# Seven homes for raw pieces from the last query job on, a top-16 over 80 of 256 pairs, and queries copied by ScalarE

## The chip, the cores and the metric

One core of one Trainium2 chip. The metric is the device time of one execution in microseconds; the kernel before was timed in three runs. The engines are TensorE (PE; its weight loads are PEld), VectorE (DVE), ScalarE (ACT), GpSimd (POOL) and SyncE (SP), each with a queue that it works through in order, and 16 DMA engines that carry the transfers of all of them.

## What is computed

A decoder layer for 256 tokens of width 1024: three gated token mixers, their merge, and a feed-forward part in which every token picks its experts by product keys. The change touches this last part. Cut to what matters:

```python
q = (hi @ w_q).reshape(B, T, 8, 2, 128)
s = einsum('bthpd,hpkd->bthpk', q, subkeys)          # 128 keys, two halves, 8 heads
s_top, i_top = top_k(s, 16)
cand = s_top[..., 0, :, None] + s_top[..., 1, None, :]          # 16 x 16 pairs
best, pos = top_k(cand.reshape(..., 256), 16)
expert = i_top[0][pos // 16] * 128 + i_top[1][pos % 16]
g = softmax(best)
a = gelu(einsum('btd,bthkd->bthk', hi, u_tab[expert]))
y = einsum('bthk,bthkd->btd', g * a, v_tab[expert])
```

`hi` is the RMS-normalised stream; both expert tables have 16384 rows of 1024 numbers (64 MB each).

## The kernel before

**Raw pieces.** Weights and both expert tables come as pieces of 128 x 1024 float32, two to a transfer of 1 MB (`load_raw`, L65 to L71, on SyncE's queue). A transfer lands in a home, a tile of the pool `rawp` with three of them. 82 pieces `w` serve the projections; each is split by ScalarE (L202) and VectorE or GpSimd (L203) into two parts, which TensorE multiplies in three products (L233 to L235). Then come 128 pieces `u` and 128 pieces `v`, which TensorE uses as they are. `ahead_split` (L260) is called before every job: it splits pieces up to two jobs ahead and issues transfers up to `more["depth"]` pieces beyond that, which is two at first.

**Queries.** The last 16 `w` jobs (66 to 81) make the queries of 8 heads x 2 halves. `ev_pq` (L828) moves each from PSUM, times the token's RMS factor. `scores` (L864) multiplies them with the keys; four at a time are copied to `sc` (L872).

**The order of the selection.** What VectorE does for the selection stands in lists `todo` of (cost, function); `tick2` and `run_todo` (L881) put a purse's worth of them into the program after each job: 1.5 in a query job, `SEL_PACE` = 1.85 in a `u` job. First all of the upper 128 tokens (t = 1), then the lower (t = 0): `top_keys` (16 of 128 keys, costed 1.4), then by rounds of heads `sel_a` (the 256 pair sums), `sel_b` (`top16` of them, costed 2.4 a head), `sel_p` (position to row and column), `sel_d` (their key numbers), and at the end `sel_c`, `sel_x` (exponential, on ScalarE), `sel_c2`, `sel_e` (transposes on TensorE). `select` (L1226) writes that list. These are no times: the purse only says where in VectorE's queue a function stands.

**Tokens in two ways.** For the upper 96 tokens the chosen rows of both tables are gathered (`x_load`, L1036, an indirect transfer of 128 rows, 512 KB, on GpSimd's queue; 96 of the first table, then 96 of the second) into six buffers, the former homes of the split parts; VectorE takes each in `x_step` (L1052: product with the token; L1057: weighted sum) and the next transfer is issued as its buffer is free. Their list has a purse of its own, `X_PACE`: 0.35 a `u` job before the gates, 1.3 after, with 1.2 as the cost of a step. For the other 160 tokens every expert is multiplied: `u_job` (L1108) makes 128 x 160 inner products of a piece `u` on TensorE, ScalarE takes their GELU; `v_job` (L1132) multiplies a piece `v` with the weights and adds up in PSUM.

**The gates.** When both halves of the selection are through, `open_gates` (L1239) gives back the room of the selection, opens three more homes (`raw2`, six in all, depth five), and from there 40 gate steps (`g_prep`, `g_gi`, `g_mm`, `g_copy`, `g_apply`) spread the chosen weights over the 128 x 160 table beside the remaining `u` jobs, at a rate of 40 steps in the jobs up to number 124.

Of the kernel before, what the change touches and what calls it, by code (L numbers as in the profile page):

```python
# [10 lines left out]
F32 = mybir.dt.float32  # L11
F32R = mybir.dt.float32r
BF = mybir.dt.bfloat16
F16 = mybir.dt.float16
I32 = mybir.dt.int32
U32 = mybir.dt.uint32
AF = mybir.ActivationFunctionType
OP = mybir.AluOpType
# [20 lines left out]
N_WARM = 12  # L39
SEL_PACE = 1.85  # L40
X_PACE = (0.35, 1.3)
RAW_BUFS = 3
# [5 lines left out]
def hybrid_block(ctx, tc, xt, memt, wst, cmpw, subk, cols, cpe, fng, ut, vt, un, out):  # L48
    nc = tc.nc
    const = ctx.enter_context(tc.tile_pool(name="const", bufs=1))  # L50
    big = ctx.enter_context(tc.tile_pool(name="big", bufs=1))
    hb = ExitStack()
    far = hb.enter_context(tc.tile_pool(name="far", bufs=1, side="right"))
    hbp = hb.enter_context(tc.tile_pool(name="hbp", bufs=1, side="right"))
    rawp = ctx.enter_context(tc.tile_pool(name="rawp", bufs=RAW_BUFS))
# [4 lines left out]

    raws, more = {}, {"from": None, "depth": RAW_BUFS - 1}

    nc.scalar.preload_act_table_set("natural_log_exp_and_others")

    def load_raw(r):  # L65
        kind, i = raw_list[r]
        pool = rawp if more["from"] is None or (r - more["from"]) // RAW_BUFS % 2 else more["pool"]
        t = pool.tile([128, 2, 1024], F32, name="raw")
        src = {"w": wst, "u": ut, "v": vt}[kind]
        nc.sync.dma_start(t, src[2 * i:2 * i + 2].rearrange("n p c -> p n c"))  # L70
        raws[r] = t  # L71
# [26 lines left out]

    nc.sync.dma_start(xT[:, 0:2], xt[:, 0:2])
    raw0 = rawp.tile([128, 2, 1024], F32, name="raw")  # L100
    raws[0] = raw0
# [724 lines left out]
    qt_ = {}  # L826

    def ev_pq(i):  # L828
        def f(p):
            qt_[i] = far.tile([128, T], F32, name=("pq0", "pq1", "rxb")[i]) if i < 3 else \  # L830
                sel.tile([128, T], F32, name=f"pq{i % 3}")
            nc.vector.tensor_tensor(qt_[i], p, rmsf[1], op=OP.mult)
        return f
# [11 lines left out]
    def norm_h(d):  # L845
# [11 lines left out]
    nc.gpsimd.iota(io2, pattern=[[1, 128], [0, 2]], base=0, channel_multiplier=0,  # L857
                   allow_small_or_imprecise_dtypes=True)
    se = ExitStack()
    sel = se.enter_context(tc.tile_pool(name="sel", bufs=1, side="right"))  # L860
# [65 lines left out]
    def sel_a(t, hs):  # L926
        if ("tf", t) not in sd:
            sel_open(t)
            nc.vector.tensor_copy(sd["tf", t], ti[t])
        sd["c", t] = sel.tile([128, len(hs), 16, 16], F32, name="cand")  # L930
        a = tv[t].rearrange("p (h s) k -> p h s k", s=2)
        for n, h in enumerate(hs):
            nc.vector.tensor_tensor(sd["c", t][:, n], a[:, h, 0, :, None].to_broadcast([128, 16, 16]),
                                    a[:, h, 1, None, :].to_broadcast([128, 16, 16]), op=OP.add)

    def sel_b(t, h, n):
        top16(sd["bv", t][:, h], sd["bi", t][:, h], sd["c", t][:, n].rearrange("p a b -> p (a b)"))

# [4 lines left out]
    def sel_p(t, hs):  # L943
        pp = sel.tile([128, 2, len(hs), 16], U32, name="pp")
        bi = some(sd["bi", t], hs)
        nc.vector.tensor_scalar(pp[:, 0], bi, 4, None, op0=OP.logical_shift_right)
        nc.vector.tensor_scalar(pp[:, 1], bi, 15, None, op0=OP.bitwise_and)
        nc.vector.tensor_copy(some(sd["pf", t], hs, 2), pp)

# [18 lines left out]
    def sel_x(t):  # L968
        nc.scalar.activation(sd["bv", t], sd["bv", t], AF.Exp)
        todo[t].append((1.1, lambda: sel_c2(t)))  # L970
# [255 lines left out]
    def select(t):  # L1226
        w = todo[t]
        for hs, parts in (X_ROUNDS if t else (((0, 1, 2, 3), 0), ((4, 5, 6, 7), 0))):
            w.append((0.35 * len(hs), lambda hs=hs: sel_a(t, hs)))
            for n, h in enumerate(hs):  # L1230
                w.append((2.4, lambda h=h, n=n: sel_b(t, h, n)))
            w.append((0.6, lambda hs=hs: sel_p(t, hs)))
            for s in range(2):
                w.append((0.1 + 0.75 * len(hs), lambda hs=hs, s=s: sel_d(t, s, hs)))
            if t:
                w.append((0.3, lambda hs=hs, parts=parts: x_index(hs, parts)))
        w.append((0.6, lambda: sel_c(t)))

    def open_gates():  # L1239
        nonlocal gp  # L1240
        se.close()
        hb.close()
        gp = ctx.enter_context(tc.tile_pool(name="gp", bufs=2))
        rc = ctx.enter_context(tc.tile_pool(name="rc", bufs=1))
        slots["RC"] = rc.tile([128, 64, ND], F32, name="RC")
        more["pool"] = ctx.enter_context(tc.tile_pool(name="raw2", bufs=RAW_BUFS))
        more["from"], more["depth"] = next_raw[0], 2 * RAW_BUFS - 1
        g_prep(0)

    gp, q, opened, rate, owed, late = None, 0, False, 0.0, 0.0, None  # L1250
    for i in range(128):
# [20 lines left out]
        if i < 4:  # L1272
            x_rows(i % 2, i > 1)
        if not opened:
            tick2(SEL_PACE if i < 90 else 1e9)
            opened = len(sel_done) == 2
            if opened:
                open_gates()
                g_gi(0)
                rate = N_G / (124.0 - i)  # L1280
# [140 lines left out]
```

## Time and profile before

| | us |
|---|---|
| median of 3 runs (lowest, highest) | 956.25 (955.26, 956.61) |
| the profiled execution, own time | 955.32 |
| its span, first to last instruction | 953.6 |
| TensorE busy | 913.3 (96%) |
| VectorE busy | 629.9 (66%) |
| ScalarE busy | 340.0 (36%) |
| GpSimd busy | 310.6 (33%) |

The span is what all times below are counted in; the rest of the profiled execution's time lies around it. TensorE's products overlap, so that its busy share says little about how fast it goes; the number of its records in a stretch says more (16 records are one `u` or `v` job). In all 285.17 MB go through the DMA engines, a mean of 299 GB/s. The granted clock of TensorE is 0.994 on average. The stages by the trace: projections and mixers up to about 260, query jobs to 308, `u` jobs to 634, `v` jobs to 930, the rest to 953.6.

### The profile page before, as it was taken

The page shows a single profiled execution, that of the slowest core. Times are in us where ns is not written, and L with a number is a line of the kernel's source. Part 1 is how long each engine was busy: PE and PEld are TensorE (multiplying, and loading weights), DVE is VectorE, ACT ScalarE, POOL GpSimd, SP SyncE. Part 2 cuts the span into 40 slices and gives each one's busy share as a digit, 9 for nine tenths or more (in the row PEclk, how much of TensorE's full clock was granted, in tenths as well). Part 3 has the DMA queues.
Part 4 walks back from the last instruction along what each step waited for, and adds up shares of the span by engine and source line. Part 5 has one row for each costly group of instructions (what it writes and reads, how often), then busy time and mean ns, then how long its engine had stood idle before and what let it go on. Part 6 is the DMA issues. An engine that isn't in the chain of part 4 may idle for free.

```text
span 953.6 us, 17339 instructions
## 1 busy us (share of the span) xinstructions
PE 913.3 (96%) x6807; PEld 870.3 (91%) x6807; DVE 629.9 (66%) x1375; ACT 340.0 (36%) x918; POOL 310.6 (33%) x343
## 2 busy tenths in 40 slices
PE   8999999998999999999999999999999998999996
PEld 6999999898999999999999989899999888888895
DVE  7757668657779969999687778874444444444412
ACT  4754679654533312113777667620000000000001
POOL 7802000026842044112344334343333333333200
PEclk9999999999999999999999999999999999999998
DMA  7644434443553499898999999999999999999951
GB/s 284 248 133 144 135 135 148 155 138 133 178 176 133 164 362 329 302 324 304 410 408 408 409 409 407 409 402 409 409 409 409 409 408 409 409 409 409 409 234 45
DMA packets 76324, 285.17 MB, mean 299 GB/s; under 512 B 6881, under 2 KB 6929, under 8 KB 75857
## 3 DMA queue, kind: packets, MB, share of 16 engines
q1 hardware_dynamic: 47152, 181.15, 50.7%
q0 software_dynamic: 28800, 102.61, 27.4%
q8 instruction: 54, 0.88, 0.4%
q10 hardware_dynamic: 288, 0.29, 0.1%
q14 instruction: 30, 0.24, 0.1%
HBM read 282.63 MB, written 1.05 MB: 297 GB/s over the span
## 4 chain that ended last, share of the span: by engine, by line
PE 48%; DMA 19%; issue 12%; DVE 10%; POOL 8%; ACT 2%; POOLq 0%; SPq 0%; DVEq 0%
DMA raw<-in_vt_dram 16%; PE po L1129 16%; POOL s L1043 7%; PE pj L233 6%; PE pj L235 6%; PE pj L234 6%; PE pj L1114 5%; DVE s L1052 1%; DMA s<-in_un_dram,xi 1%; DVE s L203 1%; ACT gi L1156 1%; POOL t L783 1%; DMA xi<-e 1%; DVE ti L902 1%; DVE sc L903 1%
## 5 line engine op out<-in xcount | busy, mean ns | idle before, releaser
L1114 PE MATMUL pj<-hA,raw 128*128 128x160 f32 x2048 | 290.3, 301 | 3.0 <-DMA raw<-in_ut_dram 2.4
L1114 PEld LDWEIGHTS pj<-hA,raw 128*128 128x128 f32 x2048 | 281.2, 191 | 7.2 <-issue 2.4
L1057 DVE SCALAR_TENSOR_TENSOR acc<-s,xw,acc 128x1024 f32<-128x1024 f32 x94 | 120.8, 1285 | 130.4 <-DMA s<-in_vt_dram,xi 124.5
L1043 POOL DMA_INDIRECT s<-in_un_dram,xi x96 | 104.4, 1087 | 187.0 <-DVE xa L1052 136.4
L1129 PE MATMUL po<-RC,raw 128*128 128x160 f32 x1024 | 148.0, 302 | 11.7 <-DMA raw<-in_vt_dram 10.6
L1129 PEld LDWEIGHTS po<-RC,raw 128*128 128x128 f32 x1024 | 140.1, 190 | 19.2 <-DMA raw<-in_vt_dram 15.9
L1129 PE MATMUL po<-RA,raw 128*128 128x160 f32 x1024 | 141.9, 300 | 3.4 <-DMA raw<-in_vt_dram 3.4
L1043 POOL DMA_INDIRECT s<-in_vt_dram,xi x96 | 91.5, 954 | 164.7 <-DVE acc L1057 152.4
L1129 PEld LDWEIGHTS po<-RA,raw 128*128 128x128 f32 x1024 | 139.4, 190 | 5.8 <-DMA raw<-in_vt_dram 5.8
L1052 DVE CUSTOM_DVE_ANT_0 s<-s,hA 128x1024 f32<-128x1024 f32 x96 | 116.9, 1221 | 29.4 <-DMA s<-in_un_dram,xi 26.4
L203 DVE TENSOR_TENSOR s<-raw,s 128x1024 fp32r<-128x1024 f32 (+1 forms) x77 | 100.9, 1316 | 28.5 <-ACT s L202 28.2
L202 ACT ACTIVATE s<-raw 128x1024 fp32r<-128x1024 f32 (+1 forms) x84 | 86.5, 1034 | 68.4 <-PE pj L234 47.1
L1156 ACT ACTIVATE gi<-oo,gv 128x128 f16<-128x128 f16 x320 | 99.3, 426 | 13.6 <-DVE oo L1145 12.7
L1204 ACT ACTIVATE RA<-pg 128x512 f32<-128x512 f32 x2 | 1.2, 593 | 281.5 <-PE pg L1306 281.5
L233 PE MATMUL pj<-hA,s 128*128 128x256 f32 x336 | 99.0, 295 | 0.1
L235 PE MATMUL pj<-hA,s 128*128 128x256 f32 x336 | 95.0, 283 | 0.0
L234 PE MATMUL pj<-hA,s 128*128 128x256 f32 x336 | 95.0, 283 | 0.0
L233 PEld LDWEIGHTS pj<-hA,s 128*128 128x128 f32 x336 | 64.3, 191 | 3.3 <-issue 1.8
L234 PEld LDWEIGHTS pj<-hA,s 128*128 128x128 f32 x336 | 64.3, 191 | 0.6 <-issue 0.5
L235 PEld LDWEIGHTS pj<-hA,s 128*128 128x128 f32 x336 | 64.2, 191 | 0.0
L1118 ACT ACTIVATE RA<-pj 128x160 f32<-128x160 f32 x64 | 19.3, 303 | 112.9 <-PE pj L1114 111.0
L781 POOL TENSOR_TENSOR t<-t,t 128x256 f32<-128x256 f32 x7 | 5.2, 736 | 106.1 <-DVE t L780 106.1
(347 smaller groups left out, 1248.7 us busy)
## 6 DMA issues: line engine op xcount, KB each, us to landing
raw<-in_ut_dram SPq DMA_DIRECT2D x64, 1024.0 KB
raw<-in_vt_dram SPq DMA_DIRECT2D x64, 1024.0 KB
raw<-in_wst_dram SPq DMA_DIRECT2D x39, 1024.0 KB
raw<-in_wst_dram SPq DMA_DIRECT2D x4, 512.0 KB
s<-in_un_dram,xi POOLq DMA_INDIRECT x96
s<-in_vt_dram,xi POOLq DMA_INDIRECT x96
x<-in_memt_dram SPq DMA_DIRECT2D x1, 1024.0 KB
cw<-in_cmpw_dram POOLq DMA_DIRECT2D x1, 1024.0 KB
```

What stands on the lines that cost most here:

```text
L202: nc.scalar.activation(a[:, c], src[:, c], AF.Copy)
L203: eng.tensor_tensor(b[:, c], src[:, c], a[:, c].bitcast(F32), op=OP.subtract)
L233: nc.tensor.matmul(dst, l1, r1, start=first, stop=False)
L234: nc.tensor.matmul(dst, l1, r2, start=False, stop=False)
L235: nc.tensor.matmul(dst, l2, r1, start=False, stop=last)
L1043: nc.gpsimd.indirect_dma_start(t, None, src, bass.IndirectOffsetOnAxis(ap=xi[:, c:c + 1], axis=0))
L1052: nc.vector.tensor_tensor_reduce(t, t, hnat[:, g], 1.0, 0.0, OP.mult, OP.add, xa[:, c:c + 1])
L1057: nc.vector.scalar_tensor_tensor(acc[:, g], t, xw[:, c:c + 1], acc[:, g], op0=OP.mult, op1=OP.add)
L1114: nc.tensor.matmul(p, a[:, k], hT[:, k, 0:ND], start=(k == 0), stop=(k == 7))
L1118: nc.scalar.activation(slot(i)[:, g:], p[:, g:], AF.Gelu)
L1129: nc.tensor.matmul(po[c // 2][:, c % 2], a[:, c * 128:c * 128 + 128], slot(i), start=(i == 0 and c % 2 == 0), stop=(i == 127), skip_group_ ...
L1156: nc.scalar.activation(gi[:, s, k // 2, :, k % 2], oo[:, k // 2, :, k % 2], AF.Copy, scale=gv[:, q, s, k:k + 1])
```

## The change

- **Homes.** `more["homes"]` is a list that turns: each transfer takes the home at its head and puts it at the end; the depth is one less than their number. Two homes of `raw2` are added once the third query is made, and two more after `u` job 0, in the room of the tiles `hB1` and `hB2`, which held the input of the query jobs. The gates open none.
- **Selection.** Of the 16 x 16 pairs (a, b) only 80 are formed: all b for a = 0, b below 8 for a = 1 to 7, b = 0 for a = 8 to 15. `sel_p` turns a position among 80 back into a row and a column with six more instructions.
- **Queries** are copied by ScalarE and not multiplied by the RMS factor; the factor is put into the exponential instead.
- **Paces and costs.** `SEL_PACE` 1.75, `X_PACE` (0.45, 1.3), and other costs for `sel_a`, `sel_b` and `sel_p`.

```diff
-SEL_PACE = 1.85
-X_PACE = (0.35, 1.3)
+SEL_PACE = 1.75
+X_PACE = (0.45, 1.3)
...
+    hbp = ctx.enter_context(tc.tile_pool(name="hbp", bufs=1, side="right"))
     hb = ExitStack()
     far = hb.enter_context(tc.tile_pool(name="far", bufs=1, side="right"))
-    hbp = hb.enter_context(tc.tile_pool(name="hbp", bufs=1, side="right"))
...
-    raws, more = {}, {"from": None, "depth": RAW_BUFS - 1}
+    raws, more = {}, {"homes": [(rawp, "raw")] * RAW_BUFS, "depth": RAW_BUFS - 1}
+
+    def add_homes(new):
+        more["homes"] = new + more["homes"]
+        more["depth"] = len(more["homes"]) - 1
...
-        pool = rawp if more["from"] is None or (r - more["from"]) // RAW_BUFS % 2 else more["pool"]
-        t = pool.tile([128, 2, 1024], F32, name="raw")
+        homes = more["homes"]
+        homes.append(homes.pop(0))
+        t = homes[-1][0].tile([128, 2, 1024], F32, name=homes[-1][1])
...
-            nc.vector.tensor_tensor(qt_[i], p, rmsf[1], op=OP.mult)
+            nc.scalar.activation(qt_[i], p, AF.Copy)
...
+    raw2 = ctx.enter_context(tc.tile_pool(name="raw2", bufs=2))
+    add_homes([(raw2, "raw")] * 2)
...
-        sd["c", t] = sel.tile([128, len(hs), 16, 16], F32, name="cand")
-        a = tv[t].rearrange("p (h s) k -> p h s k", s=2)
-        for n, h in enumerate(hs):
-            nc.vector.tensor_tensor(sd["c", t][:, n], a[:, h, 0, :, None].to_broadcast([128, 16, 16]),
-                                    a[:, h, 1, None, :].to_broadcast([128, 16, 16]), op=OP.add)
+        n = len(hs)
+        c = sel.tile([128, n, 80], F32, name="cand")
+        sd["c", t] = c
+        v = some(tv[t].rearrange("p (h s) k -> p h s k", s=2), hs)
+        nc.vector.tensor_tensor(c[:, :, 0:16], v[:, :, 0, 0:1].to_broadcast([128, n, 16]), v[:, :, 1], op=OP.add)
+        nc.vector.tensor_tensor(c[:, :, 16:72].rearrange("p h (a b) -> p h a b", b=8),
+                                v[:, :, 0, 1:8, None].to_broadcast([128, n, 7, 8]),
+                                v[:, :, 1, None, 0:8].to_broadcast([128, n, 7, 8]), op=OP.add)
+        nc.vector.tensor_tensor(c[:, :, 72:80], v[:, :, 0, 8:16], v[:, :, 1, 0:1].to_broadcast([128, n, 8]), op=OP.add)
...
-        nc.vector.tensor_scalar(pp[:, 0], bi, 4, None, op0=OP.logical_shift_right)
-        nc.vector.tensor_scalar(pp[:, 1], bi, 15, None, op0=OP.bitwise_and)
-        nc.vector.tensor_copy(some(sd["pf", t], hs, 2), pp)
+        nc.vector.tensor_scalar(pp[:, 0], bi, 3, None, op0=OP.logical_shift_right)
+        nc.vector.tensor_scalar(pp[:, 1], bi, 7, None, op0=OP.bitwise_and)
+
+        y = sel.tile([128, 6, len(hs), 16], F16, name="py")
+        row, c = y[:, 0], y[:, 1]
+        nc.vector.tensor_copy(y[:, 0:2], pp)
+        nc.vector.tensor_scalar(y[:, 2], c, 8.0, None, op0=OP.add)
+        nc.vector.scalar_tensor_tensor(y[:, 3], row, 9.0, y[:, 2], op0=OP.is_ge, op1=OP.mult)
+        nc.vector.scalar_tensor_tensor(some(sd["pf", t][:, 0], hs), row, 1.0, y[:, 3], op0=OP.subtract, op1=OP.max)
+        nc.vector.scalar_tensor_tensor(y[:, 4], row, 9.0, c, op0=OP.is_lt, op1=OP.mult)
+        nc.vector.tensor_scalar(y[:, 5], row, 1.0, 8.0, op0=OP.is_equal, op1=OP.mult)
+        nc.vector.tensor_tensor(some(sd["pf", t][:, 1], hs), y[:, 4], y[:, 5], op=OP.add)
...
-        nc.scalar.activation(sd["bv", t], sd["bv", t], AF.Exp)
+        nc.scalar.activation(sd["bv", t], sd["bv", t], AF.Exp, scale=rmsf[0][:, t:t + 1])
...
-            w.append((0.35 * len(hs), lambda hs=hs: sel_a(t, hs)))
+            w.append((0.2 + 0.1 * len(hs), lambda hs=hs: sel_a(t, hs)))
             for n, h in enumerate(hs):
-                w.append((2.4, lambda h=h, n=n: sel_b(t, h, n)))
-            w.append((0.6, lambda hs=hs: sel_p(t, hs)))
+                w.append((1.55, lambda h=h, n=n: sel_b(t, h, n)))
+            w.append((1.3, lambda hs=hs: sel_p(t, hs)))
...
-        more["pool"] = ctx.enter_context(tc.tile_pool(name="raw2", bufs=RAW_BUFS))
-        more["from"], more["depth"] = next_raw[0], 2 * RAW_BUFS - 1
...
+        if i == 0:
+            add_homes([(hbp, "hB1"), (hbp, "hB2")])
```

Three places show how instructions move; numbers after a name tell its buffers apart.

TensorE, from the first `u` jobs to the first gate step, before. Each `u` job is 8 products of `pj`; `r` and `bv` are the selected keys and weights that `sel_e` transposes, `gi` and `oo` belong to the gate step.

```order
L1114 MATMUL pj<-hA_3048,raw 128x160 x192
L985 MATMUL pg<-ident,r_3821 128x128
L985 MATMUL pg<-ident,r_3822 128x128
L985 MATMUL pg<-ident,bv_3817 128x128
L1114 MATMUL pj<-hA_3048,raw 128x160 x256
L985 MATMUL pg<-ident,r_4461 128x128
L985 MATMUL pg<-ident,r_4462 128x128
L985 MATMUL pg<-ident,bv_4457 128x128
L1114 MATMUL pj<-hA_3048,raw 128x160 x24
```

The same place now, from the first transposes on:

```order
L1010 MATMUL pg<-ident,r_3832 128x128
L1010 MATMUL pg<-ident,r_3833 128x128
L1010 MATMUL pg<-ident,bv_3828 128x128
L1139 MATMUL pj<-hA_3048,hB_4048 128x160 x16
L1139 MATMUL pj<-hA_3048,raw 128x160 x80
L1139 MATMUL pj<-hA_3048,hB_4288 128x160 x16
L1139 MATMUL pj<-hA_3048,hB_4332 128x160 x16
L1139 MATMUL pj<-hA_3048,raw 128x160 x80
L1139 MATMUL pj<-hA_3048,hB_4565 128x160 x16
L1139 MATMUL pj<-hA_3048,hB_4598 128x160 x16
L1010 MATMUL pg<-ident,r_4500 128x128
L1010 MATMUL pg<-ident,r_4501 128x128
```

The first transposes stood before job 28 and stand before job 26; the second, which open the gates, stood before job 60 (28 and 256/8 = 32 more) and stand before job 56 (30 more). Two of seven pieces lie in `hB`.

VectorE, the end of the first round (two heads), before:

```order
L905 MAX_INDEX bi_3818<-bv_3817,cand 128x8
L946 TENSOR_SCALAR pp<-bi_3818 128x32
L947 TENSOR_SCALAR pp<-bi_3818 128x32
L948 CAST pf_3819<-pp 128x4x16
L955 TENSOR_TENSOR eq<-pf_3819,io_3185 128x512
```

and now:

```order
L914 MAX_INDEX bi_3829<-bv_3828,cand 128x8
L961 TENSOR_SCALAR pp<-bi_3829 128x32
L962 TENSOR_SCALAR pp<-bi_3829 128x32
L966 CAST py<-pp 128x64
L967 TENSOR_SCALAR py<-py 128x32
L968 SCALAR_TENSOR_TENSOR py<-py 128x32
L969 SCALAR_TENSOR_TENSOR pf_3830<-py 128x2x16
L970 SCALAR_TENSOR_TENSOR py<-py 128x32
L971 TENSOR_SCALAR py<-py 128x32
L972 TENSOR_TENSOR pf_3830<-py 128x2x16
L979 TENSOR_TENSOR eq<-pf_3830,io_3188 128x512
```

Six instructions have come in between the cast and the comparison. Up to the last step of the selection VectorE's list has 14 gather steps before and 17 now.

ScalarE, three query jobs now (`s` is the first part of a split piece, `pq` the query):

```order
L209 ACTIVATE s_3238<-raw 128x1024
L839 ACTIVATE pq_3269<-pj 128x256
L209 ACTIVATE s_3274<-raw 128x1024
L839 ACTIVATE pq_3303<-pj 128x256
L881 ACTIVATE sc_3182<-pg 128x512
L881 ACTIVATE sc_3183<-pg 128x512
L209 ACTIVATE s_3315<-raw 128x1024
```

Before, the rows of `pq` were on VectorE, and ScalarE had only the others. A copy now stands between the splits of two pieces.

## Rows read from the trace of the kernel before

**Rows 1.** Windows: length, busy us (records) of PE, PEld, DVE, ACT, POOL; clock, DMA share, GB/s

```profile
268.00:308.00 40.00, 38.95 (x329) 38.63 (x328) 33.78 (x104) 13.86 (x16) 11.38 (x5) 1.00 0.46 157
...
448.80:633.70 184.90, 179.74 (x1408) 170.72 (x1409) 144.34 (x331) 127.33 (x495) 77.29 (x72) 0.99 1.03 408
633.70:729.60 95.90, 95.83 (x706) 95.59 (x704) 46.83 (x54) 1.83 (x3) 36.31 (x37) 1.00 1.02 408
729.60:903.00 173.40, 159.45 (x1107) 151.27 (x1108) 82.97 (x65) 0.00 (x0) 60.57 (x64) 1.00 1.03 409
```

**Rows 2.** Chain that ended last, in order of time: start, length, what

```profile
729.56 25.07 DMA raw<-in_vt_dram
```

**Rows 3.** DMA queues from 729.6 to 903: kind, packets, MB, share of 16 engines

```profile
q1 hardware_dynamic: 9440, 36.41, 52.7%
q0 software_dynamic: 9421, 34.30, 49.6%
```

**Rows 4.** DMA issues from the start to 633.7

```profile
s<-in_un_dram,xi POOLq DMA_INDIRECT x92
```

**Rows 5.** Waits of PE from 346 to 450: us in total, times, longest

```profile
PE pj L1114 <- DMA raw<-in_ut_dram: 2.4, 2, 1.6
```

**Rows 6.** Timeline of PE about the gates: start, length, what, idle before and releaser

```profile
446.14 0.61 PE L985 MATMUL pg<-ident,r 128*128 128x128 f32 x2
448.26 0.33 PE L985 MATMUL pg<-ident,bv 128*128 128x128 f32 x1 [1.51 <-DVE bv L977]
448.79 3.39 PE L1114 MATMUL pj<-hA,raw 128*128 128x160 f32 x23 [0.19 <-ACT RA L1118]
```

**Rows 7.** Query jobs: waits of PE from 268 to 308, and two timeline rows

```profile
PE pj L233 <- DVE pq L832: 1.0, 2, 0.8
...
294.13 2.40 POOL L203 TENSOR_TENSOR s<-raw,s 128x1024 fp32r<-128x1024 f32 x1 [2.86 <-ACT s L202]
296.80 1.06 ACT L202 ACTIVATE s<-raw 128x1024 fp32r<-128x1024 f32 x1 [2.75 <-PE pj L234]
```

**Rows 8.** Line 872: duration in ns, least, median, most; first and last start

```profile
L872 ACT ACTIVATE sc<-pg x8: 591/596/599, 273.5 to 311.6; 128x512 f32<-128x512 f32 x8
```

**Rows 9.** Timeline of DVE, first two rounds of the selection

```profile
313.94 0.28 DVE L901 MAX8 tv<-sc 128x8 f32<-128x128 f32 x1
...
315.64 0.28 DVE L901 MAX8 tv<-sc 128x8 f32<-128x128 f32 x1
...
319.38 0.75 DVE L933 TENSOR_TENSOR cand<-tv 128x256 f32<-128x256 f32 x2
320.05 0.42 DVE L901 MAX8 bv<-cand 128x8 f32<-128x256 f32 x1
...
322.44 0.41 DVE L901 MAX8 bv<-cand 128x8 f32<-128x256 f32 x1
...
324.93 0.18 DVE L946 TENSOR_SCALAR pp<-bi 128x32 uint32<-128x32 uint32 x1
325.02 0.17 DVE L947 TENSOR_SCALAR pp<-bi 128x32 uint32<-128x32 uint32 x1
325.23 0.20 DVE L948 CAST pf<-pp 128x64 f16<-128x64 uint32 x1
325.46 0.69 DVE L955 TENSOR_TENSOR eq<-pf,io 128x512 f16<-128x512 f16 x1
...
341.97 1.22 DVE L1052 CUSTOM_DVE_ANT_0 s<-s,hA 128x1024 f32<-128x1024 f32 x1 [6.55 <-DMA s<-in_un_dram,xi]
343.12 0.08 DVE L1052 DVE_READ_ACCUMULATOR2_ANT xa<- 128x1 f32 x1
```

**Rows 10.** Groups of DVE from 268 to 449: busy us, mean ns, idle before

```profile
L1052 DVE CUSTOM_DVE_ANT_0 s<-s,hA 128x1024 f32<-128x1024 f32 x15 | 18.2, 1213 | 6.6 <-DMA s<-in_un_dram,xi 6.6
```

**Rows 11.** Waits of PE from 450 to 633.7

```profile
PE pg L1167 <- ACT gi L1156: 4.1, 7, 1.0
```

**Rows 12.** DMA queue 1 from 450 to 633.7

```profile
q1 hardware_dynamic: 9824, 37.88, 51.7%
```

More of the change, by code (lines that the diff above doesn't have):

```diff
@@ L99, in hybrid_block @@
     nc.sync.dma_start(xT[:, 0:2], xt[:, 0:2])
+    more["homes"] = [(rawp, "raw")] * RAW_BUFS
     raw0 = rawp.tile([128, 2, 1024], F32, name="raw")
@@ L929, in sel_a @@
             nc.vector.tensor_copy(sd["tf", t], ti[t])
-        sd["c", t] = sel.tile([128, len(hs), 16, 16], F32, name="cand")
-        a = tv[t].rearrange("p (h s) k -> p h s k", s=2)
-        for n, h in enumerate(hs):
-            nc.vector.tensor_tensor(sd["c", t][:, n], a[:, h, 0, :, None].to_broadcast([128, 16, 16]),
-                                    a[:, h, 1, None, :].to_broadcast([128, 16, 16]), op=OP.add)
+        n = len(hs)
[7 more added lines that the diff above has]
+        nc.vector.tensor_tensor(c[:, :, 72:80], v[:, :, 0, 8:16], v[:, :, 1, 0:1].to_broadcast([128, n, 8]), op=OP.add)
     def sel_b(t, h, n):
-        top16(sd["bv", t][:, h], sd["bi", t][:, h], sd["c", t][:, n].rearrange("p a b -> p (a b)"))
+        top16(sd["bv", t][:, h], sd["bi", t][:, h], sd["c", t][:, n])
     def some(x, hs, ax=1):
```

## The prediction

> **What bounds the kernel now.** I read the stages by windows first, then the chain of waits, the DMA queues, and last the VectorE timeline. Times are microseconds from the start of the profiled execution.
>
> In the value stage (v jobs) TensorE is fed by DMA. The second window holds 706 TensorE records, 16 to a job: 44.1 jobs in 95.9 us, 2.17 us each. The third holds 1107 records, 69.2 jobs in 173.4 us, 2.51 us each, with the DMA engines at 409 GB/s [rows 1]. So 69.2 x 0.34 = 23 us are lost between 729.6 and 903, and the chain there runs through the transfer of raw pieces [rows 2]. Two queues share that rate about evenly: 36.41 MB of raw pieces (34.7 pieces of 1.05 MB, two jobs each) and 34.30 MB of gathers (65.4 gathers of 0.52 MB, one per 2.65 us) [rows 3]. At the start of the stage 92 of the 192 gathers were issued [rows 4]. The first 44 jobs ran at full speed out of the lead in the raw homes.
>
> Before that, from the opening of the gates (448.8) to 633.7, DMA is full as well, but TensorE hardly waits for it [rows 1]. Before the gates there are two waits for raw pieces, 2.4 us together [rows 5], where the first six gathers meet a prefetch only two pieces deep. At the gates TensorE itself waits: its transposes of the selection stand ready at 446.14, the last goes at 448.26 when VectorE delivers, and job 60 starts at 448.79 [rows 6]. VectorE runs its list up to there almost without a gap, so its length sets that moment.
>
> **The change, part by part. The query copies** leave VectorE for ScalarE. TensorE's waits for them there are 1.0 us [rows 7]; I take 1.0 off, with 0 and 2 as ends. ScalarE's copy is not in the trace; a 512-wide copy of the same kind costs 0.60 us [rows 8], so a 256-wide one less. ScalarE is busy 13.86 of 40 us there [rows 1], and that covers it; what it costs without cover is the slower rival.
>
> **The selection up to the gates** is a VectorE sum. A top-16 over 128 elements takes 1.70 us from start to start (313.94 to 315.64), over 256 elements 2.39 us (320.05 to 322.44) [rows 9]: 0.0054 us per element, so 80 elements take 1.44. Sixteen of them save 16 x 0.95 = 15.2 us. The pair sums cost (320.05 - 319.38)/2 = 0.335 us each, 5.4 in all; three shorter ones per round, read off by size, make 0.5 us in four rounds and 0.65 in two: 2.1 us saved. Turning positions into rows and columns takes 0.53 us a round now (324.93 to 325.46) and gains six short instructions; a short one that needs its forerunner follows it by 0.21 to 0.23 us, one that doesn't by 0.09 [rows 9]. With two of the six free, that is 1.05 us a round, 1.2 in the two wide ones: 6.6 us added.
>
> The same rows bound those six from both sides, 0.09 and 0.23 us each: 3.2 to 8.3 us. The Trainium skill, "VectorE: DVE Perf Modes", section "The TRN2 errata — SBUF-src ops pay a fixed extra latency per instruction", speaks against short instructions: an estimate by its measured fixed term of about 150 cycles is 0.19 us for 32 elements and 0.22 for 64, 7.3 us in all, and the time would come out 0.7 us higher than by the rows.
>
> Because the gather purse is filled faster, VectorE's list holds 17 gather steps before the gates where it held 14 (its last one there follows the selection [rows 10]): 3 x 1.15 us (341.97 to 343.12) = 3.5 more. At the first gather step it already waits 6.55 us for the data [rows 9]. It now gets there 2.0 us sooner, two rounds being 1.0 us shorter each (-0.17 - 1.9 + 1.05), while the index that the data wait for is only one round sooner: the wait grows by 1.0. Net: -15.2 - 2.1 + 6.6 + 3.5 + 1.0 = -6.2 us, and VectorE delivers at 448.2 - 6.2 - 1.0 = 441.0.
>
> The table now puts the gates in front of job 56 instead of 60. TensorE would arrive there at 446.1 - 4 x 2.17 - 2.4 - 1.0 = 434.0: the raw waits go, since seven homes are full when the gathers begin. So it waits about 7 us for VectorE where it waited 2, and what the homes and the copies gave is swallowed there. Job 56 starts at 441.6, job 60 at 450.3, **1.5 us later** than before. ScalarE waits too, with the exponential at the head of its queue, and the evictions of two jobs behind it; that is the same wait, not a second one. Ends: -5.5 (VectorE on time) and +6 (every short instruction at twice its price). On SyncE's queue the two transfers into the new homes hB wait for the last query product; the piece behind them is not used for five jobs, so nothing is late by it. GpSimd's queue keeps its order.
>
> **The gate steps** are the same 40, spread over 68 jobs where they had 64. Their waits on ScalarE are 4.1 us [rows 11]; I take 0.5 off, with 0 and 4.1 as ends.
>
> **The value stage.** Two things are further along when it starts. Gathers, by the table: six at the first index after job 8, then the purse over a step's cost of 1.2 for each job up to the gates and after them: before, 6 + 52 x 0.35/1.2 + 67 x 1.3/1.2 = 94 (the trace has 92); now 6 + 47 x 0.45/1.2 + 71 x 1.3/1.2 = 100.5. About 7 more are done, so the gathers end 7 x 2.65 = 18.6 us sooner; each us beside them costs TensorE 1 - 2.17/2.51 = 0.135 us: **2.5 us**. Lead: there is one more home. And before, three new homes opened at the gates on a full DMA: from 450 to 633.7 queue 1 brought 37.88 MB = 36.1 pieces [rows 12], while 67 jobs used 33.5, so the lead grew by 2.6, 0.4 short. Now the homes are full beforehand, and 71 jobs with 77 gathers ask for 77.6 MB in 192 us, 404 GB/s, which just fits. That is 1.0 to 1.4 pieces more; I take 1.3, and each is two jobs of 2.17 us: **5.6 us**. Together 8.1 off, with 3 (the lead eaten by the tight fit) and 13 as ends.
>
> Sum: +1.5 - 0.5 - 8.1 = -7.1. The profiled execution took 955.3 us (1.7 outside its span of 953.6); the median of three runs is 956.25, 0.9 above it. 955.3 - 7.1 + 0.9 = **949 us**.
>
> **Rivals.** *Faster, bytes count in full.* 7 gathers and 1.4 pieces are 5.1 MB; if the DMA stream alone sets the end they are worth 5.1/409 = 12.6 us instead of 8.1: 944.6. For it: 409 GB/s without a gap. Against: the split is even [rows 3], so raw pieces can't use what the gathers leave until the gathers end, and then TensorE, not DMA, is the bound. The Trainium skill, "DMA: Bandwidth & Descriptors", section "Queues, rings and completion order", states that each DMA engine takes turns between the queues with work, packet by packet; by that a seventh home raises no share in this stage, only the lead it starts with. Chance 0.2.
>
> *Faster, VectorE on time.* If its list is 7 us shorter than my sum (the wait for the first gather gone, the short instructions hidden), TensorE keeps 1.0 + 2.4 + 2.1 = 5.5 us instead of losing 1.5: 942. Against: the short instructions depend on each other. Chance 0.12.
>
> *No change.* VectorE's short instructions cost double and the gates come 6 us later, while the lead is worth 4 us less: 955.5 to 957. Chance 0.1.
>
> *Slower.* On ScalarE the copy of query i stands behind TensorE's last product of job i, and the split of piece i+3 behind the copy. At most 0.60 + 1.06 (ScalarE) + 2.40 (GpSimd's subtraction) [rows 7, 8] = 4.1 us pass until TensorE can use the piece, while it has two jobs of 40/13 = 3.1 us to do. Only if the split is already late by 1.5 us, as the ScalarE row that begins after waiting 2.75 us hints, does it decide; then up to 0.8 us (the nearest wait, TensorE's longest for a copy) in each of 13 jobs is 10.4 us, and 949 becomes 959. Chance 0.06.
>
> **How the numbers follow.** The forecast has 0.52. A measurement of this kernel tells about 0.2% (1.9 us) from no change. Faster by more than that: forecast and both faster rivals, 0.84, less 0.02 for the forecast's upper tail: 0.82. Same: most of no change and that tail, 0.1. Slower: its rival and the rest of no change, 0.08. The range takes the forecast's own ends and both faster rivals, 940 to 954.5; a little is left out below, and no change and slower above.
>
> **What would show it.** Right: the gates open near 441 with a TensorE wait of 5 to 9 us for VectorE in front of them; no wait for raw pieces before 600; top-16 over 80 elements near 1.44 us; v jobs start at 633 to 636; the full-speed stretch of v jobs is longer by some 10 to 20 us, and the gathers end near 885. Wrong: TensorE waiting for query pieces around 268 to 308 (slower rival); no wait at the gates (VectorE on time); v jobs at 2.51 us as long as before (the lead was not kept), or hardly any (bytes in full).

## The result and the profile after

The changed kernel takes **943.21 us** (median of 4 runs, 942.08 to 945.65); the kernel before, run beside it, 956.43 (4 runs, 955.26 to 956.74). The ratio is 0.9872, 95% interval 0.9858 to 0.9886: 12 to 13 us faster, where 7 were forecast (949.0). The profiled execution of the change took 943.12 us, 1.9 outside its span of 941.2; the span before was 953.6. As in the prediction, a raw piece below is one transfer of 1.05 MB, the work of two jobs.

By stage, from the start of the first u job (307.9, before 308.0), in the profiled executions:

| | before | forecast | after |
|---|---|---|---|
| u stage: first u job to first v job | 325.7 | +1.0 | 320.4 (-5.3) |
| v stage: first v job to the end of the span | 319.9 | -8.1 | 312.9 (-7.0) |

Windows of the kernel after, with the columns of [rows 1]:

```profile
438.70:628.30 189.60, 186.40 (x1473) 179.79 (x1473) 148.64 (x339) 128.09 (x504) 83.60 (x76) 0.98 1.01 399
628.30:748.00 119.70, 119.70 (x883) 119.70 (x882) 57.40 (x57) 1.83 (x3) 42.39 (x46) 1.00 1.03 409
748.00:880.00 132.00, 121.65 (x850) 115.63 (x848) 64.24 (x50) 0.00 (x0) 45.67 (x49) 1.00 1.03 409
```

and the chain that ended last (start, length, what):

```profile
628.50 121.72 PE po L1154 x896
750.24 29.78 DMA raw<-in_vt_dram
...
884.95 32.87 PE po L1154 x240
```

The v stage answers to [rows 1, 2] as the forecast had it. TensorE runs 896 matmuls, 56 jobs, at full speed (44 before), then 850 records of 16, 53.1 jobs, in 132 us, 2.485 us each, and the last 15 jobs from 885 on at full speed again: the gathers' queue is nearly empty by then, and VectorE's wait for the last of them ends at 889.

About the gates TensorE waits 0.77 + 2.19 us, where 7 were forecast [rows 6]:

```profile
434.86 0.27 PE L1010 MATMUL pg<-ident,r 128*128 128x128 f32 x1
435.90 0.33 PE L1010 MATMUL pg<-ident,r 128*128 128x128 f32 x1 [0.77 <-DVE r L982]
438.42 0.47 PE L1010 MATMUL pg<-ident,bv 128*128 128x128 f32 x1 [2.19 <-DVE bv L1002]
```

VectorE's list goes as costed against [rows 9], but for its last row here:

```profile
319.72 0.24 DVE L910 MAX8 bv<-cand 128x8 f32<-128x80 f32 x1
...
321.20 0.22 DVE L910 MAX8 bv<-cand 128x8 f32<-128x80 f32 x1
...
322.77 0.18 DVE L961 TENSOR_SCALAR pp<-bi 128x32 uint32<-128x32 uint32 x1
...
323.74 0.19 DVE L969 SCALAR_TENSOR_TENSOR pf<-py 128x32 f16<-128x32 f16 x1
323.85 0.18 DVE L970 SCALAR_TENSOR_TENSOR py<-py 128x32 f16<-128x32 f16 x1
323.95 0.17 DVE L971 TENSOR_SCALAR py<-py 128x32 f16<-128x32 f16 x1
...
324.24 0.69 DVE L979 TENSOR_TENSOR eq<-pf,io 128x512 f16<-128x512 f16 x1
...
337.61 1.23 DVE L1077 CUSTOM_DVE_ANT_0 s<-s,hA 128x1024 f32<-128x1024 f32 x1 [4.29 <-DMA s<-in_un_dram,xi]
```

A top-16 over 80 elements takes 1.48 us (forecast 1.44), turning positions into rows and columns 1.47 (0.53 + 1.05 = 1.58 forecast). But the wait for the first gather is 4.3 us, where 6.6 became 7.6 in the forecast.

### The profile page after: what moved, and what is told of

Read it like the earlier page. It is cut to its first block, busy times and chain, and to the rows that moved or that the text cites. A ratio compares the mean times of both kernels' runs of the same rounds, so it can differ in the third digit from the quotient of the medians.

```text
span 941.2 us, 17393 instructions
## 1 busy us (share of the span) xinstructions
PE 907.9 (96%) x6807; PEld 871.6 (93%) x6807; DVE 609.9 (65%) x1398; ACT 344.4 (37%) x940; POOL 309.7 (33%) x343
## 3 DMA queue, kind: packets, MB, share of 16 engines
HBM read 282.63 MB, written 1.05 MB: 301 GB/s over the span
## 4 chain that ended last, share of the span: by engine, by line
PE 56%; DMA 17%; DVE 15%; issue 4%; ACT 4%; POOL 3%; SPq 0%; POOLq 0%; DVEq 0%
PE po L1154 19%; DMA raw<-in_vt_dram 13%; PE pj L1139 7%; PE pj L240 7%; PE pj L241 7%; PE pj L242 7%; DMA s<-in_un_dram,xi 3%; DVE s L1077 3%; ACT gi L1181 3%; POOL s L1068 2%; DVE eq L979 1%; DVE r L982 1%; POOL t L790 1%; PE pg L1192 1%; PE z L241 1%
## 5 line engine op out<-in xcount | busy, mean ns | idle before, releaser
L1139 PE MATMUL pj<-hA,raw 128*128 128x160 f32 x1472 | 210.6, 303 | 0.0
L1139 PEld LDWEIGHTS pj<-hA,raw 128*128 128x128 f32 x1472 | 204.2, 192 | 1.4 <-PE pg L1192 1.0
L1154 PE MATMUL po<-RC,raw 128*128 128x160 f32 x704 | 101.8, 302 | 6.5 <-DMA raw<-in_vt_dram 6.1
L1154 PE MATMUL po<-RA,raw 128*128 128x160 f32 x768 | 105.7, 299 | 1.7 <-DMA raw<-in_vt_dram 1.7
L1154 PEld LDWEIGHTS po<-RC,raw 128*128 128x128 f32 x704 | 96.4, 190 | 11.4 <-DMA raw<-in_vt_dram 10.0
L1154 PEld LDWEIGHTS po<-RA,raw 128*128 128x128 f32 x768 | 104.7, 190 | 2.2 <-DMA raw<-in_vt_dram 2.1
L1139 PE MATMUL pj<-hA,hB 128*128 128x160 f32 x576 | 82.1, 300 | 0.0
L1139 PEld LDWEIGHTS pj<-hA,hB 128*128 128x128 f32 x576 | 78.9, 190 | 1.0 <-ACT ga L1146 0.3
```

The lines of the kernel that those rows point to most:

```text
L1139: nc.tensor.matmul(p, a[:, k], hT[:, k, 0:ND], start=(k == 0), stop=(k == 7))
L1154: nc.tensor.matmul(po[c // 2][:, c % 2], a[:, c * 128:c * 128 + 128], slot(i), start=(i == 0 and c % 2 == 0), stop=(i == 127), skip_group_ ...
```

## The experiments

Twelve kernels ran, in three lots. Each lot had its own runs of the kernel before (medians 956.1, 955.0 and 954.8), and the ratios are to those. The stages are taken as above, from each profiled execution; the first u job starts at 306.5 to 309.2 in them, even where the code ahead of it is the same, so stages are compared by length. "Gathers" are those issued by the first v job. Each row's stages are of one execution. Three pairs of runs differ only in how pieces of the v stage are issued; their u stages are 320.4 and 322.8 (the change, two_queues), 316.8 and 316.2 (xpace_old, tq_x35), 308.0 and 309.3 (x35_12, quarter_x35_12). So 2 us in the u stage of two executions decide nothing; the v stage repeats better (312.9, 313.1 and 312.8 in the change, copies_back and index_late).

| run | us | ratio (95%) | u job 0 to v job 0 | v job 0 to end | gathers |
|---|---|---|---|---|---|
| before | 956.43 | 1 | 325.7 | 319.9 | 92 |
| the change | 943.21 | 0.9872 (0.9858 to 0.9886) | 320.4 | 312.9 | 99 |
| no_homes | 954.35 | 0.9985 (0.9972 to 0.9999) | 327.3 | 317.8 | 99 |
| sel256 | 942.87 | 0.9862 (0.9846 to 0.9878) | 319.0 | 315.5 | 92 |
| copies_back | 945.61 | 0.9887 (0.9872 to 0.9903) | 319.3 | 313.1 | 99 |
| xpace_old | 939.49 | 0.9834 (0.9817 to 0.9851) | 316.8 | 314.2 | 95 |
| homes6 | 947.02 | 0.9919 (0.9904 to 0.9933) | 320.6 | 317.3 | 99 |
| x11 | 937.40 | 0.9811 (0.9797 to 0.9824) | 311.9 | 316.2 | 88 |
| two_queues | 937.73 | 0.9824 (0.9809 to 0.9839) | 322.8 | 306.5 | 99 |
| tq_x35 | 939.51 | 0.9841 (0.9827 to 0.9854) | 316.2 | 312.2 | 95 |
| index_late | 945.77 | 0.9907 (0.9888 to 0.9926) | 323.8 | 312.8 | 99 |
| x35_12 | 934.25 | 0.9793 (0.9773 to 0.9813) | 308.0 | 317.2 | 90 |
| x35_11 | 939.10 | 0.9831 (0.9815 to 0.9846) | 307.8 | 323.6 | 84 |
| quarter_x35_12 | 938.99 | 0.9832 (0.9816 to 0.9847) | 309.3 | 320.8 | 90 |

### Which part carries the gain

**no_homes** takes the homes out and keeps the rest of the change:

```
-    raw2 = ctx.enter_context(tc.tile_pool(name="raw2", bufs=2))
-    add_homes([(raw2, "raw")] * 2)
...
-            add_homes([(hbp, "hB1"), (hbp, "hB2")])
```

(and, as before, `open_gates` opens three more).

> The change without its homes: three homes until the gates and three more from there, selection over 80 pairs, ScalarE's copies and the new paces kept. Theory of the forecast (a home is worth the jobs in its piece): 1.3 pieces less lead, two jobs of 2.17 us each, so the v stage is 5.6 us longer; the raw waits of 2.4 us come back near the first gathers, but are swallowed by the 2.2 us that TensorE waits for VectorE at the gates: 948 to 950. Rival, bytes in full: 1.3 pieces of 1.05 MB at 409 GB/s, 3.3 us: 946.5. Rival, the homes did nothing and the selection did it all: 943.

Measured 954.35: the selection, the copies and the paces without the homes are worth almost nothing, and neither the theory nor a rival had the homes at 11 us. The stages say where: 4.9 us in the v stage (the forecast's 5.6), and 6.9 in the u stage, where the forecast gave them nothing.

**sel256** keeps homes and copies and goes back to 256 pairs, with the old costs and paces:

```
-SEL_PACE = 1.75
-X_PACE = (0.45, 1.3)
+SEL_PACE = 1.85
+X_PACE = (0.35, 1.3)
...
-        c = sel.tile([128, n, 80], F32, name="cand")
+        sd["c", t] = sel.tile([128, len(hs), 16, 16], F32, name="cand")
```

> The change with the old selection, costs and paces: seven homes and ScalarE's copies kept. Theory of the forecast: VectorE's list is as long as before, the gates open in front of job 60 near 445 to 448, v jobs start at 631 to 634 instead of 628.3, and 7 to 8 gathers fewer are done by then, worth 2.5 to 2.9 us: 948.5 to 952. Rival, VectorE's saving counts in full (15.2 + 2.1 - 6.6 = 10.7 us): 954. Rival, the homes did all: 943 to 944.5.

Measured 942.87, the same as the change: against the theory, and with the rival that the homes did all. The selection's saving on VectorE and the seven gathers that come of the new pace take 2.6 us off the v stage (0.37 each, where 0.36 had been worked out), and the u stage gives 1.4 of it back (within the noise). So the selection and its paces, together, are worth nothing that can be measured here.

**copies_back** puts the query copies back on VectorE (and takes the RMS factor out of the exponential again, which is not shown):

```
-            nc.scalar.activation(qt_[i], p, AF.Copy)
+            nc.vector.tensor_tensor(qt_[i], p, rmsf[1], op=OP.mult)
```

> The change with the sixteen query copies back on VectorE (with the RMS factor in them). Theory: TensorE's waits of 1.0 us in the query stage come back, but VectorE decides when the gates open, and its last group of scores came only 0.1 us sooner with the copies gone: 943 to 943.5, no difference. Rival, carried through to the end: 944.2. Rival, ScalarE's copies delay the splits: 942 or less.

Measured 945.61, with an interval that overlaps the change's; the profiled spans are 941.6 and 941.2. TensorE's 1.0 us of waits for the copies are back in the trace, and its last transpose at the gates starts 1.1 us later than in the change (439.56 and 438.42); but the change's clock fell there and this execution's did not (last section), so that the equal spans may be luck in part. What the copies are worth stays open, between nothing and some 2 us.

**xpace_old** has only the first pace back:

```
-X_PACE = (0.45, 1.3)
+X_PACE = (0.35, 1.3)
```

> The change with the gather steps before the gates at the old pace of 0.35 us a job: 4 gathers fewer are issued when v jobs begin, and 3 gather steps of 1.15 us fewer stand on VectorE in front of the gates. Theory (TensorE's wait at the gates is VectorE's length): the waits of 3.0 us there go, the gathers end 4 x 2.65 = 10.6 us later in the v stage, at 0.135 us each is 1.4 us: 943.2 - 3.0 + 1.4 = 941.6. Rival, the wait at the gates is made good later, by DMA: 944.6. Rival, bytes in full: 4 gathers of 0.52 MB at 409 GB/s are 5.1 us, 945.3.

Measured 939.49, faster than the change: the u stage is 3.6 us shorter, with no wait at the gates, and four gathers fewer cost the v stage 1.3. The three gather steps that the new pace put in front of the gates did harm. Against sel256, which has the same first pace, the selection over 80 pairs is then worth 3.4 us (942.87 to 939.49; the intervals just overlap), and the new pace used that up.

### Where the homes gained in the u stage

From the gates on, the run without the homes has 5.6 to 6 us more for the same 72 jobs and 40 gate steps. Its windows and queues there (kind, packets, MB, share), then the waits of VectorE, ScalarE and TensorE (total, times, longest):

```profile
438.40:634.00 195.60, 189.01 (x1473) 182.10 (x1473) 149.75 (x340) 128.27 (x504) 81.98 (x77) 0.97 1.02 405
...
q1 hardware_dynamic: 10366, 39.98, 51.4%
q0 software_dynamic: 10711, 39.02, 50.4%
...
DVE s L1067 <- DMA s<-in_un_dram,xi: 12.2, 19, 1.8
...
ACT gi L1171 <- DVE oo L1160: 18.6, 11, 3.1
...
PE pg L1182 <- ACT gi L1171: 6.1, 8, 1.5
```

The kernel after, in 189.6 us:

```profile
q0 software_dynamic: 10682, 38.92, 52.5%
q1 hardware_dynamic: 9450, 36.42, 48.4%
...
DVE s L1077 <- DMA s<-in_un_dram,xi: 5.7, 11, 1.5
...
ACT gi L1181 <- DVE oo L1170: 11.4, 11, 2.7
...
PE pg L1192 <- ACT gi L1181: 2.8, 6, 1.0
```

I read the three waits as one chain; the next two runs test that. VectorE works its list in order, so a gather step whose rows have not come also holds up the gate matrices (`oo`) behind it; ScalarE waits for these, TensorE for ScalarE's `gi`. The gathers are late because three new homes fill at the gates: 39.98 MB of raw pieces instead of 36.42 through a DMA at 405 GB/s. **homes6** tests that: as many homes as no_homes has from the gates on, but full before the gathers begin.

```
-            add_homes([(hbp, "hB1"), (hbp, "hB2")])
+            add_homes([(hbp, "hB1")])
```

> The change with six homes, hB2 left out: as many as the run without its homes has after the gates (954.35 us), but all of them filled before the gathers fill the DMA. Theory now (from the gates to the first v job the DMA moves 400 to 408 GB/s, so the three pieces that are loaded at the gates push out the gathers, VectorE waits for rows, ScalarE for VectorE, TensorE for ScalarE): three pieces of 1.05 MB at 408 GB/s are 7.7 us, so v jobs start 6 to 7.7 us sooner than there and the v stage is as long as there: 946.5 to 948.5; the seventh home is then worth the rest, two jobs of 2.17 us. Rival, lead alone (the forecast's view: filling late cost 0.4 of a piece): 952.5. Rival, the seventh home carries most of the gain: 951 or more.

Measured 947.02, as the theory had it (its rivals had 951 and more). Its window and queues:

```profile
438.40:628.40 190.00, 185.20 (x1474) 178.30 (x1474) 149.30 (x339) 128.16 (x504) 80.31 (x76) 0.99 1.02 400
...
q0 software_dynamic: 10722, 39.05, 52.6%
q1 hardware_dynamic: 9510, 36.66, 48.4%
```

The u stage is 6.7 us shorter than without the homes, 5.6 of it from the gates on (190.0 and 195.6), the v stage as long (317.3 and 317.8). TensorE's listed waits for gate matrices differ by 2.0 of the 5.6 (4.1 us here, 6.1 without the homes); its clock fell once here, at the gates, and three times without the homes (last section), and how the rest comes about is not shown. The seventh home is then worth 317.3 - 312.9 = 4.4 us, two jobs of 2.17, all of it in the v stage.

**x11** makes room on the DMA from the other side, with fewer gather steps after the gates:

```
-X_PACE = (0.45, 1.3)
+X_PACE = (0.45, 1.1)
```

> The change with 1.1 us of gather steps a job after the gates in place of 1.3: 12 gathers fewer are issued when v jobs begin. Theory (the gate steps wait for late gathers through VectorE and ScalarE): with 6.3 MB less to move there the DMA is no longer full, TensorE's waits for the gate matrices (2.8 us) and the drop of its clock near 550 (1.7 us) go, v jobs start at 622 to 625 instead of 628.3; the v stage is 12 x 0.36 = 4.3 us longer: 941 to 945, no difference on the whole. Rival, the gate waits have nothing to do with the gathers: v jobs start at 628 and the time is 947.5. Rival, bytes in full: 12 x 1.28 us = 15 us out of one stage and into the other, v start 613 or as far as TensorE allows.

Measured 937.40, below the theory's 941 to 945. Neither VectorE nor TensorE shows a wait of that chain from 439 to 620, and the u stage is 8.5 us shorter, where the waits and the drop of the clock made 4.5; eleven gathers fewer cost the v stage 3.3. So the gate steps did wait for gathers. From the gates to the first v job it takes 180.9 us, with TensorE busy for 180.7 of them, so the rival's "as far as TensorE allows" fits the size better than the sum of the listed waits: why 4 us more went than these is not shown.

```profile
439.20:620.10 180.90, 180.68 (x1473) 176.40 (x1473) 135.87 (x318) 126.77 (x504) 67.10 (x66) 1.00 1.01 393
```

### The first index

The wait for the first gather (4.3 us, not 7.6) was the other miss. GpSimd issues the index and then the first gathers; SyncE's raw piece is issued next to it. Before:

```profile
329.75 1.11 POOL L1009 DMA_DIRECT2D xi<-e  x2 [33.23 <-DVE e L1013]
337.46 1.05 POOL L1043 DMA_INDIRECT s<-in_un_dram,xi  x1 [6.60 <-PE pj L1114]
...
330.09 0.37 SPq L70 DMA_DIRECT2D raw<-in_ut_dram  x1
```

After:

```profile
328.53 1.10 POOL L1034 DMA_DIRECT2D xi<-e  x2 [30.23 <-DVE e L1038]
332.03 1.05 POOL L1068 DMA_INDIRECT s<-in_un_dram,xi  x1 [2.39 <-DMA xi<-e]
...
329.95 0.37 SPq L76 DMA_DIRECT2D raw<-in_ut_dram  x1
```

Issued 0.34 us ahead of the raw piece, the index (two transfers of 4 KB) lets the first gather start 7.7 us after it; issued 1.42 ahead, 3.5 us after it. (TensorE is named as the releaser before, but the products that this gather waits for are those of the query jobs, long done; that it was the index is inferred from the change, where the index is named.) The other runs fall in the same two cases: 0.34 ahead in sel256, GpSimd idle for 6.5 us; 1.4 ahead in ten runs, idle for 2.2 to 2.4. **index_late** moves it on purpose, by short copies in a chain:

```
+        if hs == (0, 4):
+            dm = sel.tile([128, 2, 16], F32, name="dm")
+            nc.vector.tensor_copy(dm[:, 0], sd["r", 1, 0][:, 0])
+            for k in range(5):
+                nc.vector.tensor_copy(dm[:, (k + 1) % 2], dm[:, k % 2])
```

> The change with six short VectorE copies in a chain ahead of the first index, which hold it up by 1.2 to 1.4 us. Theory (where the 4 KB index goes out 0.35 us or less ahead of a 1 MB raw piece its transfer stands behind it and takes 6.5 us; 1.4 us ahead of it takes 2.3): the first gather is issued 4.2 us later than the copies alone make it, near 337.5 instead of 332.0, VectorE waits some 8.5 us for its rows instead of 4.3, and delivers at the gates near 443.5 instead of 438.4; TensorE waits 8 us there instead of 3; 946 to 948.5. Rival, the index takes 2.3 us wherever it stands: the first gather at 333.4, the gates at 439.8, 944.5.

```profile
328.51 1.10 POOL L1034 DMA_DIRECT2D xi<-e  x2 [31.30 <-DVE e L1043]
335.30 1.05 POOL L1073 DMA_INDIRECT s<-in_un_dram,xi  x1 [5.68 <-DMA xi<-e]
...
328.93 0.37 SPq L76 DMA_DIRECT2D raw<-in_ut_dram  x1
```

The first u job starts 1.0 us sooner in this run, so the index is issued 1.0 us later than in the change, and 0.42 us ahead of the raw piece. The first gather comes 4.3 us later, counted from the first u job. So in all fourteen kernels the delay goes with the lead over the raw piece; what the index waits for in the DMA is not shown. The price, 945.77, is just under the 946 to 948.5 expected: TensorE's wait splits into 3.3 us in front of the first transposes and 1.5 in front of the second.

### The v stage's two queues

**two_queues** issues every second raw piece of the v stage on ScalarE's queue:

```
-        nc.sync.dma_start(t, src[2 * i:2 * i + 2].rearrange("n p c -> p n c"))
+        eng = nc.scalar if kind == "v" and i >= 7 and i % 2 else nc.sync
+        eng.dma_start(t, src[2 * i:2 * i + 2].rearrange("n p c -> p n c"))
```

> The change with every second raw piece of the v stage issued on ScalarE's DMA queue instead of SyncE's. Theory (every queue with work gets an equal share, so the raw pieces get half of 409 GB/s beside the gathers, 204, while v jobs of 2.17 us want 241): with two queues of raw pieces beside one of gathers they may take 273, v jobs run at 2.17 us throughout, 628.3 + 128 x 2.17 = 906 instead of 931.8, and the gathers, 95 of 0.52 MB, take the remaining 168 GB/s and all of it at the end, done near 892: about 919 to 922. Rival, gathers last: they get too little, VectorE's last gather steps come at 920 to 925, 935 to 938. Rival, the share doesn't go by queue: 943.

Measured 937.73: "gathers last". From 748 to 880, in the kernel after:

```profile
q1 hardware_dynamic: 7185, 27.69, 52.3%
q0 software_dynamic: 7184, 26.16, 50.0%
```

and in two_queues, with its window and the chain's end:

```profile
748.00:880.00 132.00, 132.00 (x974) 132.00 (x973) 53.52 (x42) 1.28 (x1) 38.68 (x41) 1.00 1.03 409
...
q0 software_dynamic: 6046, 22.02, 42.0%
q1 hardware_dynamic: 4165, 16.08, 30.4%
q10 hardware_dynamic: 4101, 15.75, 29.9%
...
902.60 6.53 DMA s<-in_vt_dram,xi
```

The share does go by queue: two of them bring 31.8 MB, 241 GB/s, which is all that v jobs of 2.17 us use, and TensorE is busy throughout. But the total stays 409 GB/s, so the gathers end at 909 instead of 889, and TensorE stands waiting for them, 8.2 us. The theory had them done near 892, with all of the rate to themselves at the end; from 896.7 to 909, where theirs is the only queue that moves data, they get 317 GB/s:

```profile
q0 software_dynamic: 1075, 3.89, 85.8%
...
PE pg L1327 <- DVE acc L1083: 8.2, 1, 8.2
```

**tq_x35** has the old first pace as well (the two edits above together):

> The same two queues, and the old pace of 0.35 us of gather steps a job before the gates, which had 939.5 us alone. Theory: both gains add up, 24 us of the v stage off 939.5: 915 to 918. Rival, gathers last: four more of them are left, 937. Rival, the share doesn't go by queue: 939.5.

Measured 939.51, no better than xpace_old alone: with four gathers more left over, again the gathers come last.

### A version that beats both

**x35_12**, **x35_11** and **quarter_x35_12** put the findings together: no gather step too many before the gates, and fewer after them.

```
-X_PACE = (0.45, 1.3)
+X_PACE = (0.35, 1.2)
```

(x35_11: 1.1; quarter_x35_12: 1.2, and `i % 4 == 1` in place of `i % 2` in the line above.)

> The change with gather steps at 0.35 us a job before the gates and 1.2 after: 92 gathers are issued when v jobs begin, 90 in the run with 0.45 and 1.1 (937.4 us). Theory: no wait at the gates (2.1 to 3.0 us there), most of the waits for late gathers gone: 934 to 936.5. Rival, the gates' wait is made good by DMA, which is what bounds: 937 to 938.

> The change with gather steps at 0.35 us a job before the gates and 1.1 after: 86 gathers are issued when v jobs begin. Theory: TensorE waits neither at the gates nor for gate matrices, v jobs start near 617 to 618; four gathers more than with 0.45 and 1.1 are left to the v stage, where they are already last with five jobs behind them, so that they begin to count in full, 2 to 5 us: 936 to 939. Rival, each still costs 0.36 us: 935.5.

> Gather steps at 0.35 and 1.2 us a job, and every fourth raw piece of the v stage on ScalarE's DMA queue. Theory: raw pieces get some 57% of the DMA instead of half, v jobs are fed better, the gathers end later but not after the jobs: 930 to 934. Rival, the gathers come last as with every second piece there (937.7): 936 to 938.

x35_12 has the lowest median, 934.25 us, 0.9793 of the kernel before (0.9773 to 0.9813), as its theory had it. It is clear of the change and of xpace_old; its runs (933.30 to 937.51) overlap those of x11 and of two_queues. Its u stage from the gates on:

```profile
433.50:614.40 180.90, 180.67 (x1473) 176.40 (x1473) 142.05 (x329) 126.78 (x504) 73.88 (x72) 1.00 1.02 405
...
DVE s L1077 <- DMA s<-in_un_dram,xi: 3.1, 7, 0.8
```

The same 72 jobs and 40 steps that take 189.6 us in the change take 180.9, with TensorE busy for all but 0.2 of it and the DMA still full. x35_11 shows the point from which it turns: its u stage is no shorter (307.8), since TensorE bounds it now, and six gathers fewer cost the v stage 6.4 us, 1.07 each instead of 0.37. These are the slowest of five executions of x35_11 and the fastest of five of x35_12; by the medians it is 4.9 us, 0.8 each. Its chain ends in gathers:

```profile
896.87 15.28 DMA s<-in_vt_dram,xi
```

quarter_x35_12 (938.99) missed its 930 to 934 by the same rule: v jobs are well fed, and the gathers come last, done at 907, with TensorE waiting 22 us for them.

## Why the prediction was right, and where it was off

The time came out 6 us under the forecast. The v stage's term was right; the two of the u stage, the gates and the gate steps, were both put too high (together +1.0 forecast, -5.3 measured). Of its signs two did not come: a wait of 5 to 9 us at the gates (it was 3.0) and v jobs from 633 to 636 (628.3).

- **The v stage**: right. 7.0 us of the 8.1. The gathers' price (7 x 0.37 = 2.6 by sel256) and the home's (4.4 by homes6) were the terms of the sum; 1.3 pieces of lead, 5.6, was slightly high. That TensorE loses by its share of an even split was shown by two_queues: a second queue raised the raw pieces' part from 27.69 to 31.83 MB in 132 us, where a home did not raise it (36.41 MB in 173.4 us before [rows 3] and 27.69 in 132 after are both 210 GB/s). This agrees with the Trainium skill, "DMA: Bandwidth & Descriptors", section "Queues, rings and completion order": each DMA engine takes turns between the queues that have work.
- **The gates**: the step that failed is "the wait grows by 1.0" for the first gather. It shrank from 6.6 to 4.3 us, since the index was now issued 1.42 us ahead of a raw piece and not 0.34. The forecast took the transfer's time for fixed and moved only its start; 441.0 less the 3.3 us is 437.7, and VectorE delivered at 438.4. The rest of the VectorE sum held: the six short instructions added 0.94 us to a round (1.47 - 0.53), where the rows gave 1.05. Those that need no forerunner started 0.10 to 0.11 us behind the one before. By the Trainium skill's fixed term ("VectorE: DVE Perf Modes", section "The TRN2 errata — SBUF-src ops pay a fixed extra latency per instruction") they would have cost more than by the rows, an estimated 7.2 us in all (the prediction has 7.3): the 0.19 us that this gives for 32 elements is about what one lasts here (0.17 to 0.19 us), but not what each adds.
- **The gate steps**: the step that failed is "I take 0.5 off", which looked at TensorE's own wait for ScalarE and took the fill of the homes for lost lead. From the first job after the gates to the first v job the forecast has 193.1 us, measured 189.6. The three pieces loaded there take 7.7 us of a full DMA; filling six homes ahead of that instead of there took 5.6 us off (no_homes to homes6). That it goes through VectorE's place in line is what the waits and x11 show.
- **The selection and the copies**: that their gain would be swallowed was right in sum (sel256 is as fast), not in its working: the swallowing was put at 7 us of waiting at the gates, which were 3. What swallowed it is the pace: with the old one there is no wait at the gates, and the selection is worth 3.4 us (xpace_old).
- **The rivals**: both faster ones came nearer to the time than the forecast (944.6 and 942 for 943.2), by luck. "Bytes count in full" put 12.6 us in the v stage, where a gather counts 0.37 us and not 1.28 until the gathers are last (x35_11, 0.8 to 1.07), and nothing among the gate steps, where 5.6 us of 7.7 showed. "VectorE on time" had its place right, but not its size (3.3 us of the 7). Neither "no change" nor the slower rival on ScalarE showed: TensorE is busy for all 40 us from 268 to 308.

## What to carry to other kernels

Where an engine with its work in order serves both a transfer and a critical step, a late transfer blocks that engine, and the step behind it, though the critical engine itself never waits for DMA. A full DMA alone does no harm: at 405 GB/s x35_12 lost nothing there. So count bytes for each stage against the DMA's rate and move transfers (here three prefetched pieces) into the stage where it has room. Then shift bulk work between stages until the two streams end together; its price rises from a share (0.37 us a gather) towards the whole (0.8 to 1.07 of 1.28) once it is the last to end.

## What was not expected of the hardware

A small transfer's time depended on a microsecond: GpSimd waited 2.2 to 2.4 us for an index (two transfers of 4 KB) that it had issued 1.4 us ahead of a 1 MB piece, and 5.7 to 6.6 us where it had issued it 0.34 to 0.42 us ahead. Nothing between the two was tried.

And TensorE's granted clock fell after some of its waits. Two windows of the kernel after, the first about its waits of 0.77 and 2.19 us at the gates, the second behind waits of 1.4 us in all for gate matrices from 538 to 549:

```profile
436.00:444.00 8.00, 5.81 (x32) 5.62 (x33) 7.69 (x17) 4.53 (x13) 3.56 (x3) 0.79 0.90 331
544.00:556.00 12.00, 10.81 (x72) 10.03 (x71) 8.49 (x21) 7.32 (x29) 3.97 (x4) 0.86 1.03 408
```

and the same windows of x35_12, which has no such waits:

```profile
436.00:444.00 8.00, 8.00 (x65) 7.96 (x64) 4.17 (x10) 6.13 (x23) 4.07 (x3) 1.00 1.02 401
544.00:556.00 12.00, 11.98 (x102) 11.76 (x100) 9.71 (x23) 9.22 (x37) 5.14 (x5) 1.00 1.01 403
```

0.79 over 8 us and 0.86 over 12 are each 1.7 us of full speed lost (the two levels are 2.4 and 1.2 GHz). The run without the homes has three such drops among its gate steps, the kernel before one (at 552), the change one and another at the gates, sel256 and x35_12 none. What decides is not shown. The 1.5 us at the gates before [rows 6] had no drop behind it, and copies_back, which waits 0.79 and 2.19 us at the gates as the change does, keeps its clock:

```profile
436.00:444.00 8.00, 5.03 (x37) 4.58 (x35) 7.80 (x18) 4.63 (x14) 2.78 (x3) 1.00 0.99 326
```

Nor is it shown that a drop lengthens the run by as much. xpace_old has one among its gate steps and tq_x35, which is the same up to there, has none; they take 189.8 and 189.2 us from the gates to the first v job.
